# Seven-product MLP of a Hymba-style encoder block: a step's second weight load issued in its middle, shorter waits before the sums made ahead, four copies on ScalarE, and the third step's forms begun later

## The chip, the cores and the metric

The kernel runs on one core of one Trainium2 chip. The metric is device time in microseconds (us) of one execution. The kernel before took 2946.3 us (median of 3 runs, 2946.01 to 2948.02).

A core has five engines with a queue of instructions each, worked off in order: PE (TensorE: matrix products; its weight loads are listed apart as PEld), DVE (VectorE), ACT (ScalarE), POOL (GpSimd) and SP (SyncE, which here only issues transfers). An instruction that has to wait for another engine or a transfer holds up all that stands behind it in its own queue. Products are summed in PSUM banks; all other tiles lie in SBUF; "DRAM" is the chip's main memory.

## The reference, cut to what matters

The block mixes tokens (attention and a recurrent unit), adds the input, and then runs a gated MLP with a width-3 convolution along the sequence between its two projections. All numbers are float32. The change lies in the MLP:

```python
    h = rms_norm(x, norm2_g[l])                        # x: 2048 x 1024
    u = depthwise_conv(h @ w_up[l], up_conv_w[l], up_conv_b[l], 1, 1)   # w_up: 1024 x 6144
    gate, val = jnp.split(u, 2, axis=-1)
    x = x + (jax.nn.gelu(gate) * val) @ w_down[l]      # w_down: 3072 x 1024
return rms_norm(x, final_g)
```

## The kernel before, in words

**Seven products instead of eight.** Both projections are computed two blocks by two with seven block products in place of eight (a Strassen-like scheme). Each product takes sums and differences of the blocks as its operands, and its result is added to several blocks of the output. Every operand is held as two parts, a rounded one and the rest, so that a product is three passes of PE: high by high, high by low, low by high. Such a pair is a "form". `split` makes it: ACT writes the high part (line 142) and DVE subtracts (line 147).

**Steps.** There are 72 steps, i = 0 to 71. Steps 0 to 47 are the up-projection: 24 pairs of 128 columns (gate and value) for the second half of the sequence (steps 0 to 23) and for the first half (24 to 47; step 24 takes the forms of step 23, so nothing is loaded or formed for it). Steps 48 to 71 are the down-projection: three thirds q of the inner dimension, eight row pairs each. A step has seven *slots*, one for each product, of 12 matmuls each (four k by three passes), 84 in all (`mms`, line 1404). Products 0 to 3 have PSUM banks of their own; 4, 5 and 6 are added onto banks 0, 3 and 2 (`own = {4: 0, 5: 3, 6: 2}`). In slot 4 DVE adds bank 3 to an output block (`add(v2c, v2c, b[3])` in `step`, `add(x22, x22, b[3])` in `down`, both line 1485). PE's slot 5 writes onto bank 3 again, so its first matmul waits for this add.

**What a slot issues.** Behind its matmuls a slot queues, in this order: one piece of the step before (`before`: convolution, gelu, product, store), its own additions, one form of the next step (`nxt`, generator `a_forms`), and one piece of side work (`side`). An engine's queue is just the order of this code; nothing is reordered later.

**Forms of the next step.** Step i's weights (in the down-projection: the stored activations) come in two raw tiles, one for the columns of gate and one for those of value; a pool of three buffers (`rawp`) holds them. `load_w(i + 2)` is a generator that issues the first tile's load, yields, and issues the second's. Each goes out on SP's queue and waits there until its buffer is free. Steps i and i+2 need four tiles and the pool has three, so the second load of step i+2 waits until a_forms(i+1) has read its first tile for the last time: with the form of slot 4 in an up step, of slot 2 in a down step. POOL makes the sums of the raw tiles (lines 1314, 1316, 1318, 1322); the first of them reads the second tile.

**Side work.** The fixed operands also need sums. `sums_ahead` makes them from four loaded blocks of 128x512: it issues four loads, waits n slots, makes one sum a slot on DVE in four slots (lines 1596 to 1602), issues four stores two slots later, and ends: n + 8 slots in all. With n = 6 that is 14 slots, exactly two steps. There are four of these for the rows of the activations (names `h_d`, `t_d`) and twelve for the down-projection's weights (`in_w_down`, `wt_d`). They are chained from step 2 on (the four, then five) and from step 24 on (the other seven).

**Seams.** Where the fixed operand changes (steps 23, 47, 55 and 63) 28 forms are made anew during the step, four a slot (`remake`, tiles `fb<-rg`). They come through a ring of nine buffers (`load_ring`, tile `rg`). Nine loads are issued a step ahead; each further one is issued right behind a form, into the buffer which that form has freed.

**The first seam** is the start of the MLP: `emit_h2(0)` transposes the last rows on PE in four goes and copies each result out in two halves (ACT line 1219, DVE line 1220). The transposes have one PSUM buffer, so each waits for the copies of the one before.

The names of the page: `pu` is a bank of products, `fa` and `fb` are forms, `raw` the raw tiles, `s` POOL's sums, `y` and `u` the convolution's tiles, `x_t` a tile of the residual in the down-projection, `st` and `tp` the copies and transposes of `emit_h2`.

## Time and profile before

| | before |
|---|---|
| median of 3 runs | 2946.3 us |
| the profiled execution: time | 2942.63 us |
| its span, first to last instruction | 2940.8 us |
| mean granted TensorE clock | 0.979 |
| busy: PE, DVE, ACT, POOL | 2761.9, 2225.2, 1524.1, 710.5 us |
| first matmul of the MLP (tile `pu`) | 1410.1 us after the span's start |
| last one | starts at 2931.2 us |

The MLP is the second half of the span, 1521 us. Lines of a timeline read: start in us, duration in us, engine, line, operation, tiles out<-in, shapes, count, and in brackets how long the engine had been idle before and what ended that. "SPq" and "ACTq" are transfers being issued; the duration of such a row includes the waiting between the first and the last of its group. Lines of a list of waits read: who waited, for whom, total us, how many times, the longest.

### The profile page before, as it was taken

The page shows a single profiled execution, that of the slowest core. Times are in us where ns is not written, and L with a number is a line of the kernel's source. Part 1 is how long each engine was busy: PE and PEld are TensorE (multiplying, and loading weights), DVE is VectorE, ACT ScalarE, POOL GpSimd, SP SyncE. Part 2 cuts the span into 40 slices and gives each one's busy share as a digit, 9 for nine tenths or more (in the row PEclk, how much of TensorE's full clock was granted, in tenths as well). Part 3 has the DMA queues.
Part 4 walks back from the last instruction along what each step waited for, and adds up shares of the span by engine and source line. Part 5 has one row for each costly group of instructions (what it writes and reads, how often), then busy time and mean ns, then how long its engine had stood idle before and what let it go on. Part 6 is the DMA issues. An engine that isn't in the chain of part 4 may idle for free.

```text
span 2940.8 us, 34037 instructions
## 1 busy us (share of the span) xinstructions
PE 2761.9 (94%) x12016; PEld 2185.9 (74%) x12016; DVE 2225.2 (76%) x2954; ACT 1524.1 (52%) x2308; POOL 710.5 (24%) x576
## 2 busy tenths in 40 slices
PE   8998998999999999999799999989999979989898
PEld 6666786777777777777577777777777857868687
DVE  6766676888888888556778777787877777776776
ACT  5777534777777777434443434454444443232443
POOL 5224433111111111010032322212222223323221
PEclk9999998999999999999999999999999989989999
DMA  3233352111111111577333443444342245555653
GB/s 130 95 128 119 94 166 96 38 48 53 47 50 46 51 53 38 174 256 236 109 129 119 132 128 123 136 144 143 109 143 101 83 142 176 189 190 184 222 159 115
DMA packets 234171, 359.89 MB, mean 122 GB/s; under 512 B 30928, under 2 KB 119888, under 8 KB 233872
## 3 DMA queue, kind: packets, MB, share of 16 engines
q1 hardware_dynamic: 210960, 298.98, 32.4%
q10 hardware_dynamic: 23040, 58.73, 5.3%
q8 instruction: 94, 1.54, 0.2%
q14 instruction: 77, 0.63, 0.1%
HBM read 231.34 MB, written 118.42 MB: 119 GB/s over the span
## 4 chain that ended last, share of the span: by engine, by line
PE 54%; DVE 16%; DMA 6%; issue 4%; ACT 2%; SPq 1%; ACTq 0%; POOL 0%; DVEq 0%; POOLq 0%
PE pu L1404 31%; DVE u L1519 4%; PE mx L815 4%; PE s L975 4%; PE s L974 4%; PE b L1013 4%; PE b L1011 4%; PE a L1001 4%; DVE fa L147 2%; DMA b<-in_w_down 2%; PE po L1164 2%; DVE y L1485 2%; DVE fb L147 1%; SPq L90 1%; DMA l<-lru_d 1%
## 5 line engine op out<-in xcount | busy, mean ns | idle before, releaser
L1404 PE MATMUL pu<-fb,fa 128*128 128x512 f32 x6027 | 1412.5, 396 | 95.7 <-DVE y L1485 62.8
L1404 PEld LDWEIGHTS pu<-fb,fa 128*128 128x128 f32 x6027 | 1139.2, 190 | 366.9 <-DVE y L1485 73.0
L820 DVE TENSOR_REDUCE mxt<-mx 128x2 f32<-128x1024 f32 x244 | 298.3, 1223 | 82.0 <-PE mx L815 81.5
L1314 POOL TENSOR_TENSOR s<-raw 128x512 f32<-128x512 f32 x70 | 97.9, 1399 | 1038.8 <-DMA raw<-in_w_up 677.3
L984 ACT ACTIVATE phi<-s 128x1024 fp32r<-128x1024 f32 x256 | 263.2, 1028 | 153.3 <-PE s L975 145.9
L991 DVE TENSOR_TENSOR plo<-p,phi 128x1024 fp32r<-128x1024 f32 x256 | 332.1, 1298 | 7.9 <-ACT p L985 7.9
L147 DVE TENSOR_TENSOR fa<-raw,fa 128x512 fp32r<-128x512 f32 (+1 forms) x284 | 244.3, 860 | 100.7 <-ACT fa L142 99.7
L1519 DVE SCALAR_TENSOR_TENSOR u<-y,ucw_s,u 128x1024 f32<-128x1024 f32 (+1 forms) x192 | 264.5, 1378 | 1.7
L142 ACT ACTIVATE fa<-raw 128x512 fp32r<-128x512 f32 (+1 forms) x284 | 175.9, 620 | 171.3 <-PE pu L1404 90.1
L985 ACT ACTIVATE p<-s 128x1024 f32<-128x1024 f32 x256 | 261.3, 1021 | 0.5 <-DVE plo L991 0.3
L974 PE MATMUL s<-qa,ka 128*128 128x512 f32 x512 | 203.2, 397 | 4.2 <-ACT p L985 2.6
L975 PE MATMUL s<-qb,kb 65*128 65x512 f32 x512 | 203.5, 397 | 0.0
L147 DVE TENSOR_TENSOR fa<-s,fa 128x512 fp32r<-128x512 f32 (+1 forms) x213 | 157.9, 741 | 43.0 <-ACT fa L142 43.0
L1541 ACT ACTIVATE u<-u 128x1024 f32<-128x1024 f32 (+1 forms) x48 | 51.0, 1062 | 255.2 <-DVE u L1519 255.2
L815 PE MATMUL mx<-ka,qa 128*128 128x512 f32 x512 | 167.5, 408 | 11.9 <-DVE mxt L820 4.9
L1485 DVE TENSOR_TENSOR y<-pu,u 128x512 f32<-128x512 f32 x144 | 99.3, 690 | 102.6 <-PE pu L1404 102.4
L1164 PE MATMUL po<-wo_hi,m 128*128 128x512 f32 x512 | 167.2, 403 | 4.5 <-ACT fb L1029 3.7
L1528 ACT ACTIVATE u<-y,ucb_s,ucw_s 128x1024 f32<-128x1024 f32 (+1 forms) x96 | 119.2, 1242 | 98.9 <-DVE y L1485 97.1
L815 PEld LDWEIGHTS mx<-ka,qa 128*128 128x128 f32 x512 | 139.5, 310 | 40.0 <-DVE mxt L820 8.7
L142 ACT ACTIVATE fa<-s 128x512 fp32r<-128x512 f32 (+1 forms) x213 | 132.5, 622 | 57.0 <-PE pu L1404 31.9
L1013 PE MATMUL b<-phi,ones_r 128*65 128x512 f32 x512 | 161.2, 396 | 0.0
L1001 PE MATMUL a<-phi,vt 128*128 128x512 f32 x512 | 160.6, 395 | 0.0
(248 smaller groups left out, 4173.1 us busy)
## 6 DMA issues: line engine op xcount, KB each, us to landing
raw<-in_w_up SPq DMA_DIRECT2D x94, 512.0 KB
raw<-g_d SPq DMA_DIRECT2D x192, 128.0 KB
x_t<-x_d SPq DMA_DIRECT2D x96, 256.0 KB
x_t<-in_x SPq DMA_DIRECT2D x44, 512.0 KB
l<-lru_d SPq DMA_DIRECT2D x32, 512.0 KB
x_d<-x_t ACTq DMA_DIRECT2D x64, 256.0 KB
g_d<-u ACTq DMA_DIRECT2D x24, 512.5 KB
b<-in_w_down SPq DMA_DIRECT2D x48, 256.0 KB
```

Source lines behind the costliest of these rows:

```text
L142: ACT.activation(out=hi, in_=src, func=AF.Copy)
L147: e_lo.tensor_tensor(out=lo, in0=src, in1=f32(hi), op=ALU.subtract)
L815: PE.matmul(ps, lhsT=qa[u].rearrange("p (q t) -> p t q", t=4)[:, qt], rhs=ka[group(u)][:, kc * 512:(kc + 1) * 512], start=True, stop=True)
L820: DVE.tensor_reduce(out=mxt[u % 2][:, qt, 2 * kp:2 * kp + 2], in_=pair, axis=AX.X, op=ALU.max)
L974: PE.matmul(ps[:, h], lhsT=ka[g][:, keys], rhs=qa[u], start=True, stop=False)
L975: PE.matmul(ps[:, h], lhsT=kb[g][:, keys], rhs=qb[u], start=False, stop=True)
L984: ACT.activation(out=p_hi, in_=ps, func=AF.Exp)
L991: DVE.tensor_tensor(out=p_lo, in0=p, in1=f32(p_hi), op=ALU.subtract)
L1001: PE.matmul(pa[u], lhsT=vt[:, kt, group(u), 0:128], rhs=p_hi[:, h], start=kt == 0, stop=kt == 15)
L1013: PE.matmul(pb[u], lhsT=ones_r[:, 0:65], rhs=p_hi[:, h], start=False, stop=i == 7 and h == 1)
L1404: PE.matmul(ps, lhsT=lh, rhs=rh, start=start and n == 0, stop=stop and n == 2, skip_group_check=more)
L1519: DVE.scalar_tensor_tensor(out=u[:, 0:w], in0=y[:, o:o + w], scalar=ucw_s[:, t * FT + f, o:o + 1], in1=u[:, 0:w], op0=ALU.mult, op1=ALU.add)
```

## The change

Five edits:

1. `step`: `load_w(i + 2)` issues its first load at the step's start as before, and its second one in slot 4, behind that slot's form and ahead of its piece of side work.
2. `down`: the same in slot 3.
3. The twelve `sums_ahead` of the down-projection's weights wait n = 4 slots instead of 6; the four of the rows keep 6.
4. `emit_h2(0)`: both halves are copied by ACT; for the other row blocks nothing changes.
5. In step 1 the forms of step 2 begin three slots later; those that are left over come behind the step.

```diff
@@ emit_h2
                 ACT.activation(out=t[:, 0], in_=tp[:, 0], func=AF.Copy, scale=g2_s[:, k0:k0 + 1])
-                DVE.tensor_scalar(t[:, 1], tp[:, 1], g2_s[:, k0 + 1:k0 + 2], None, ALU.mult)
+                if v:
+                    DVE.tensor_scalar(t[:, 1], tp[:, 1], g2_s[:, k0 + 1:k0 + 2], None, ALU.mult)
+                else:
+                    ACT.activation(out=t[:, 1], in_=tp[:, 1], func=AF.Copy, scale=g2_s[:, k0 + 1:k0 + 2])
@@ step
-            run(load_w(i + 2))
+            ld = load_w(i + 2)
+            next(ld, None)
...
                 next(nxt, None)
+                if slot == 4:
+                    run(ld)
                 next(side, None)
@@
-        sums_w = [sums_ahead(down_srcs(n), wt_d[n], 6) for n in (8, 9, 10, 11, 4, 5, 6, 7, 0, 1, 2, 3)]
+        sums_w = [sums_ahead(down_srcs(n), wt_d[n], 4) for n in (8, 9, 10, 11, 4, 5, 6, 7, 0, 1, 2, 3)]
@@ down
-            run(load_w(i + 2))
+            ld = load_w(i + 2)
+            next(ld, None)
...
                 next(nxt, None)
+                if j == 3:
+                    run(ld)
                 next(side, None)
@@ the loop over the steps
-            nxt = a_forms(i + 1)
+            nxt = chain(wait(3), a_forms(2)) if i == 1 else a_forms(i + 1)
```

SP's queue in step 55, the seam between the first and the second third of the down-projection (`raw<-g_d` are quarters of a raw tile, `rg` ring loads):

```order
 L90 DMA raw<-g_d_119 128x2x128
 L90 DMA raw<-g_d_120 128x2x128
-L90 DMA raw<-g_d_121 128x2x128
-L90 DMA raw<-g_d_122 128x2x128
-L90 DMA raw<-g_d_123 128x2x128
-L90 DMA raw<-g_d_124 128x2x128
 L90 DMA rg<-wt_d_102 128x512
 L90 DMA rg<-wt_d_103 128x512
```

```order
-L90 DMA rg<-in_w_down 128x512 x8
+L90 DMA rg<-in_w_down 128x512 x5
+L90 DMA raw<-g_d_121 128x2x128
+L90 DMA raw<-g_d_122 128x2x128
+L90 DMA raw<-g_d_123 128x2x128
+L90 DMA raw<-g_d_124 128x2x128
+L90 DMA rg<-in_w_down 128x512 x3
```

The second raw tile's four loads stood ahead of all ring loads of the step and now stand behind twelve of them. In steps 23 and 47 (`step`, slot 4) the second load comes behind sixteen.

DVE's queue where the first sums of the weights are made, with n = 6 before (`t` and `b` are the sums, lines 1596 to 1602; `y_12721<-pu,y_12721` is the add of bank 3 in slot 4; of the change, the lines 1602 to 1608 and 1488 are the same instructions):

```order
L147 TENSOR_TENSOR fa<-raw,fa 128x512
L1596 TENSOR_TENSOR t_14306<-b 128x512
L1519 SCALAR_TENSOR_TENSOR u_12723<-y_12721,ucw_s,u_12723 128x1024 x2
L147 TENSOR_TENSOR fa<-s,fa 128x512
L1598 TENSOR_TENSOR b<-b 128x512
L1485 TENSOR_TENSOR u_12724<-pu,u_12724 128x512
L1519 SCALAR_TENSOR_TENSOR u_12722<-y_12720,ucw_s,u_12722 128x1024
L147 TENSOR_TENSOR fa<-raw,fa 128x512
L1600 TENSOR_TENSOR b<-t_14306,b 128x512
L1519 SCALAR_TENSOR_TENSOR u_12722<-y_12720,ucw_s,u_12722 128x1024
L1485 TENSOR_TENSOR y_12721<-pu,u_12724 128x512
L147 TENSOR_TENSOR fa<-s,fa 128x512
```

and of the change:

```order
L147 TENSOR_TENSOR fa<-s,fa 128x512
L1602 TENSOR_TENSOR t_14261<-b 128x512
L1488 TENSOR_TENSOR y_12720<-pu,u_12724 128x512
L147 TENSOR_TENSOR fa<-raw,fa 128x512
L1604 TENSOR_TENSOR b<-b 128x512
L1488 TENSOR_TENSOR y_12721<-pu,u_12724 128x512
L147 TENSOR_TENSOR fa<-raw,fa 128x512
L1606 TENSOR_TENSOR b<-t_14261,b 128x512
L1522 SCALAR_TENSOR_TENSOR u_12723<-y_12721,ucw_s,u_12723 128x1024 x2
L147 TENSOR_TENSOR fa<-s,fa 128x512
L1608 TENSOR_TENSOR b<-b 128x512
L1488 TENSOR_TENSOR u_12724<-pu,u_12724 128x512
```

Before, all four sums stand in slots 0 to 3 of a step, ahead of the add in slot 4. Now the first two stand in slots 5 and 6 of one step and the other two in slots 0 and 1 of the next. Since a chain link is 12 slots long instead of 14, the place moves two slots towards the step's start from link to link.

ACT's queue in step 1, before (`fa` are the forms of step 2, lines 1525 and 1528 the convolution of step 0, 1488 copies of a bank):

```order
L1488 ACTIVATE u_12724<-pu 128x512
L142 ACTIVATE fa<-s 128x512
L1525 ACTIVATE sv<-y_12721 128x2
L1528 ACTIVATE u_12723<-y_12721,ucb_s,ucw_s 128x1024
L142 ACTIVATE fa<-raw 128x512
L142 ACTIVATE fa<-s 128x512
L1525 ACTIVATE sv<-y_12720 128x2
```

and of the change:

```order
L1491 ACTIVATE u_12724<-pu 128x512
L1528 ACTIVATE sv<-y_12721 128x2
L1531 ACTIVATE u_12723<-y_12721,ucb_s,ucw_s 128x1024
L142 ACTIVATE fa<-raw 128x512
L1528 ACTIVATE sv<-y_12720 128x2
L1531 ACTIVATE u_12722<-y_12720,ucb_s,ucw_s 128x1024
L142 ACTIVATE fa<-s 128x512
```

The form of POOL's first sum (`fa<-s`) stood ahead of the convolution's two activations and now stands behind both.

## The prediction

> **What bounds the kernel now.** I read the page's engines first, then PE's waits, then PE's matmuls on `pu` in slices of 20 us, then the timeline at each stall.

> ```profile
> PE 2761.9 (94%) x12016; PEld 2185.9 (74%) x12016; DVE 2225.2 (76%) x2954; ACT 1524.1 (52%) x2308; POOL 710.5 (24%) x576
> PE pu L1404 <- DVE y L1485: 62.8, 19, 20.2
> PE pu L1404 <- DVE x_t L1485: 29.5, 3, 14.6
> 1540.00:1560.00 20.00, 18.38 (x81) 1.00 0.32 103
> 1560.00:1580.00 20.00, 20.00 (x89) 1.00 0.45 140
> 2400.00:2420.00 20.00, 4.45 (x20) 0.72 0.56 183
> 1490.76 19.18 PEld L1404 LDWEIGHTS pu<-fb,fa 128*128 128x128 f32 x84 [0.23 <-DVE y L1485]
> ```

> In the MLP PE is the bound: slices without a stall are full (20.00 of 20.00), and a step of 84 matmuls takes 19.2 us. What the change can win is PE's stalls, all behind adds on DVE (line 1485): 62.8 + 29.5 = 92.3 us. So for each stall the question is what made that add late. They fall into three kinds, with their rows below: one in about every second up step, one at each seam, one in step 1.

> **Sums of the weights (n = 4).** A step with four sums, then one without:

> ```profile
> 1496.59 0.69 DVE L1485 TENSOR_TENSOR y<-pu,u 128x512 f32<-128x512 f32 x1 [1.47 <-PE pu L1404]
> 1500.47 1.30 DVE L1596 TENSOR_TENSOR t<-b 128x512 f32<-128x512 f32 x1 [0.41 <-DMA b<-h_d]
> 1510.81 0.68 DVE L1602 TENSOR_TENSOR b<-b 128x512 f32<-128x512 f32 x1
> 1511.41 0.68 DVE L1485 TENSOR_TENSOR y<-pu,y 128x512 f32<-128x512 f32 x1
> 1512.14 10.19 PE L1404 MATMUL pu<-fb,fa 128*128 128x512 f32 x43 [1.79 <-DVE y L1485]
> 1864.65 0.69 DVE L1485 TENSOR_TENSOR y<-pu,u 128x512 f32<-128x512 f32 x1 [1.47 <-PE pu L1404]
> 1877.04 0.68 DVE L1485 TENSOR_TENSOR y<-pu,y 128x512 f32<-128x512 f32 x1
> ```

> The first `y<-pu,u` waits for the old step's last matmul and so marks the step's start; `y<-pu,y` is the add of slot 4. From one to the other's end: 1512.09 - 1496.59 = 15.50 with sums, 1877.72 - 1864.65 = 13.07 without. So a sum costs 2.43/4 = 0.61. PE wants the bank 60/84 of a step in, 13.7: a slack of 0.6 without sums, a stall of about 1.8 with four. The stall of 1.79 agrees.

> Of the 19 waits for `y`, three are seams (7.59, 6.13 and 20.15, quoted below); the other 16 make 62.8 - 33.9 = 28.9, or 1.81 each: 4 for the rows, 12 for the weights. Sums in slots 4 to 6 stand behind the add; DVE idles there (1.47 in the row above), so I count them as free. Their cost if that cover is gone: 0.61 each. With links of 12 slots a link starts in slot 0, 5, 3, 1, 6, 4, 2, and sums come 5 to 8 slots later, so 2, 1, 3, 3, 1, 2, 4 of the four lie in slots 0 to 3. At 0.61 less 0.6 that is 0.6, 0, 1.2, 1.2, 0, 0.6, 1.8. The five of the first half keep 3.0, the seven of the second 5.4: 8.4 in place of 12 x 1.81 = 21.7. **Gain 13**, bounds 5 (the backlog is carried into the next step) and 20. The rows keep n = 6 and their slots; only the 0.41 wait for `b` goes: **gain 1**, bounds -1 and 3.

> **The second load in the middle, up steps without a seam.**

> ```profile
> 1491.38 0.33 SPq L90 DMA_DIRECT2D raw<-in_w_up  x1
> 1491.75 2.20 SPq L90 DMA_DIRECT2D b<-h_d  x4
> 1495.59 1.30 POOL L1314 TENSOR_TENSOR s<-raw 128x512 f32<-128x512 f32 x1 [15.47 <-DMA raw<-in_w_up]
> 1496.97 1.29 POOL L1316 TENSOR_TENSOR s<-s,raw 128x512 f32<-128x512 f32 x1
> 1499.85 0.62 ACT L142 ACTIVATE fa<-s 128x512 fp32r<-128x512 f32 x1
> ```

> The second load goes out at 1491.38, 14 us into its step, when the form of slot 4 frees the buffer; the side's loads were queued in slot 0 and go out right behind. So the new place changes nothing for the second load, and the side's loads go out some 14 us sooner, which gives back more than n = 4 takes (two slots, 5.5 us). I cost it at 0. The cover: POOL's second sum ends at 1498.27 and ACT wants it at 1499.85, 1.6 us of room. Past that each us of delay is a us on DVE.

> **Seams of steps 47, 55 and 63.**

> ```profile
> 2407.87 3.98 SPq L90 DMA_DIRECT2D rg<-wt_d  x7
> 2411.87 1.32 ACT L142 ACTIVATE fb<-rg 128x512 fp32r<-128x512 f32 x2 [11.04 <-DMA rg<-wt_d]
> 2412.53 1.38 DVE L147 TENSOR_TENSOR fb<-rg,fb 128x512 fp32r<-128x512 f32 x2 [6.03 <-ACT fb L142]
> 2415.23 0.69 DVE L147 TENSOR_TENSOR fb<-rg,fb 128x512 fp32r<-128x512 f32 x1 [1.32 <-ACT fb L142]
> 2424.61 21.60 PE L1404 MATMUL pu<-fb,fa 128*128 128x512 f32 x83 [20.15 <-DVE y L1485]
> 2448.19 2.11 PE L1404 MATMUL pu<-fb,fa 128*128 128x512 f32 x8 [1.76 <-DVE x_t L1485]
> 2574.98 2.49 DVE L147 TENSOR_TENSOR fb<-rg,fb 128x512 fp32r<-128x512 f32 x4
> 2586.93 0.69 DVE L147 TENSOR_TENSOR fb<-rg,fb 128x512 fp32r<-128x512 f32 x1 [7.12 <-ACT fb L142]
> 2588.85 1.36 DVE L147 TENSOR_TENSOR fb<-rg,fb 128x512 fp32r<-128x512 f32 x2 [1.23 <-ACT fb L142]
> 2591.93 5.71 DVE L147 TENSOR_TENSOR fb<-rg,fb 128x512 fp32r<-128x512 f32 x4
> 2592.10 1.65 POOL L1314 TENSOR_TENSOR s<-raw 128x512 f32<-128x512 f32 x1 [23.11 <-DMA rg<-in_w_down]
> 2598.30 13.94 PE L1404 MATMUL pu<-fb,fa 128*128 128x512 f32 x49 [14.59 <-DVE x_t L1485]
> 2758.08 0.69 DVE L147 TENSOR_TENSOR fb<-rg,fb 128x512 fp32r<-128x512 f32 x1 [6.84 <-ACT fb L142]
> 2768.68 26.52 PE L1404 MATMUL pu<-fb,fa 128*128 128x512 f32 x103 [13.15 <-DVE x_t L1485]
> ```

> In step 47 the ring loads go out only at 2407.87, behind the second raw load, which waits for slot 2's form. ACT then waits 11.04 for the tenth ring tile, and DVE idles 6.03 + 1.32 = 7.35. Moved behind the ring loads, the raw load no longer holds them up; a ring load goes out nine forms (over two slots) before its own form, and the first landed 4.0 after its issue (2407.87 to 2411.87). So DVE's idle time goes.

> Step 47: DVE stays the bound through slot 4 of step 48, where PE waits 1.76 again. The stall in 47 shrinks by about 10, that in 48 grows, and together they win DVE's idle time. **Gain 7**, bounds 3 and 11.

> Step 55: idle 7.12 + 1.23 = 8.35. Besides, the four forms of slot 3 took 5.71 while POOL was summing, against 2.49 without: 3.2 more. POOL will start later than those forms, since the raw load now lands behind twelve ring loads. The add comes 8.35 + 3.2 = 11.6 sooner, the stall falls from 14.6 to 3.0. The 3.2 return in slots 4 to 6 and may cost about 1 in step 56. **Gain 10.5**, bounds 6 and 14. Step 63 is alike: 6.84 + 0.5 + 3.2 = 10.5 of 13.15. **Gain 10**, bounds 6 and 13.

> The clock: after 20.15 us without work 83 matmuls took 21.60, 2.4 more than a step's 19.2, at a granted 0.72; after stalls of 1.8 it stayed at 1.00. I leave this out of the sum, as a stall of 3 lies between. [...]

> **Step 23.**

> ```profile
> 1923.17 23.05 PE L1404 MATMUL pu<-fb,fa 128*128 128x512 f32 x90 [6.13 <-DVE y L1485]
> 1905.90 3.29 DVE L147 TENSOR_TENSOR fb<-rg,fb 128x512 fp32r<-128x512 f32 x4 [1.93 <-ACT fb L142]
> ```

> The ring wasn't held up here (its second raw buffer is free early). The raw load moves behind sixteen ring loads, and POOL's sums from slot 0 (3.29 instead of 2.49) to the seam's end. **0**: 0.8 won, as much lost later; bounds -3 and 1.

> **The first seam and step 1.**

> ```profile
> 1426.43 0.48 DVE L1220 TENSOR_SCALAR st<-tp,g_s 128x256 f32<-128x256 f32 x1
> 1426.96 1.11 PE L1216 MATMUL tp<-idn,x_t 128*128 128x128 f32 x4 [4.94 <-DVE st L1220]
> 1460.17 0.63 ACT L142 ACTIVATE fa<-s 128x512 fp32r<-128x512 f32 x1 [4.81 <-POOL s L1316]
> 1460.83 1.11 DVE L147 TENSOR_TENSOR fa<-s,fa 128x512 fp32r<-128x512 f32 x1 [5.08 <-ACT fa L142]
> 1469.38 11.00 PE L1404 MATMUL pu<-fb,fa 128*128 128x512 f32 x38 [7.59 <-DVE y L1485]
> ```

> PE waits 4.94 for DVE's half of a copy (1426.43); ACT's second copy would follow its first, some 2.5 sooner, for 0.5 more of ACT each. **Gain 2**, bounds 0 and 3. In step 1 ACT waits 4.81 for POOL with the convolution queued behind, DVE 5.08, and PE 7.59. With the forms three slots later the convolution goes first, and about 5.5 of the 7.59 go; three forms (1.8 on DVE) then lie ahead of step 2, and its second raw load waits for one of them. **Gain 5**, bounds 1 and 7.

> **Sum.** 13 + 1 + 7 + 10.5 + 10 + 0 + 2 + 5 = 48.5. From the profiled execution's 2942.6: 2894.1. That run lies 3.7 below the median of 2946.3, so the forecast is 2898.

> **Rivals.**
> - *The sums merely move their stall.* DVE works nearly without a pause in a side step; a sum in slots 5 and 6 could delay the next step's add. Against it: the idle 1.47, and the step after each one with sums makes no stall. Gain 0 in place of 13: 2911.
> - *The seams stay bound.* 28 forms of 0.6 us each are work for DVE all the same, and the ring could be late for its own reasons. For it: the stall of 6.13 in step 23, where nothing holds up the ring. Against it: DVE's idle 7 to 8 us. A third of 27.5 is left: 2916.
> - *Slower: the second load is late.* It now queues in SP behind the side's stores, which wait for DVE's sums, and loads, which wait for those stores. The place: up steps 2 to 36 in which both are emitted in slots 0 to 3. It decides once those are held until more than 1.6 us past the buffer's release, 14 us into the step. In about ten such steps a load 8 us late (the time from the issue of four `b` at 1491.75 to the first sum) costs 6.4 each, 64, less the seams' and step 1's 35: 2975. Against it: their sums stand a slot or more ahead of the form that frees the buffer, so the wait is over first. [...]
> - *The clock returns.* If PE keeps its full clock after a stall of 3, as it does after 1.8, the 2.4 us lost after a long one are saved at 55 and at 63: 2893.

> **Chances.** Forecast 0.58, sums 0.10, seams 0.12, clock 0.12, slower 0.08. Range 2882 to 2924: the independent bounds of the terms (about 12 either way around 48.5), stretched to take in the first two rivals and a mix of them; without them 2886 to 2910. What a measurement can tell from no change is about 0.2%, 6 us. Only the slower case and a sliver of the mixes lie outside "faster": 0.90, same 0.03, slower 0.07.

> **What would show it.** Right: no DVE idle behind ring loads in the seams, stalls of about 10 and 6 in steps 47 and 48 and about 3 in 55 and 63; in the second half of the up steps stalls of 0 to 1.8 that differ from link to link, in the rows' steps still 1.8; a stall of about 2 in step 1. Wrong: ACT waiting for POOL's `s` in up steps (the load is late); `rg` still named as releaser in the seams; stalls of 1.8 in every link, or small ones in every step.

## The result, and the profile after

The changed kernel takes 2912.9 us (median of 4 runs, 2911.99 to 2916.96) where the kernel before takes 2946.2 us on the same chip (4 runs, 2944.01 to 2948.02): a ratio of 0.989, 95% interval 0.9873 to 0.9907. The forecast was 2898, with a range of 2882 to 2924. So it is faster, and inside the range, but only 33 of the 48.5 us came. The time is outside 2886 to 2910, the bounds of the terms alone, and nearer to two of the rivals (2911 and 2916) than to the forecast; whether one of them was at work has to be read from the stretches below.

The profiled execution of the changed kernel took 2917.0 us, with a span of 2915.2. The busy times from its page and the list of PE's waits (who waited for whom, total us, times, longest):

```profile
PE 2770.3 (95%) x12016; PEld 2191.9 (75%) x12016; DVE 2232.0 (77%) x2950; ACT 1525.6 (52%) x2312; POOL 713.6 (24%) x576
```

```profile
PE pu L1407 <- DVE y L1488: 43.9, 21, 9.8
PE pu L1407 <- DVE x_t L1488: 17.7, 5, 5.3
```

The lines of the changed kernel are three higher: 1407 are the matmuls, 1488 DVE's adds, 1317 to 1325 POOL's sums, 1522 the taps of the convolution. PE's waits for these adds went from 62.8 + 29.5 = 92.3 us to 61.6.

**Where the time went.** ScalarE copies bank 0 once in every step (`u<-pu`, 72 of them), so these copies are a ruler along the program. From the timeline of the kernel before, the first matmul into `pu` and the copies of the steps 5, 23, 25, 47, 49, 57 and 71:

```profile
1410.11 1.61 PE L1404 MATMUL pu<-fb,ax 128*128 128x512 f32 x6 [0.87 <-DVE x_t L1170]
...
1540.07 0.60 ACT L1488 ACTIVATE u<-pu 128x512 f32<-128x512 f32 x1 [0.17 <-PE pu L1404]
...
1907.34 0.57 ACT L1488 ACTIVATE u<-pu 128x512 f32<-128x512 f32 x1
1953.14 0.60 ACT L1488 ACTIVATE u<-pu 128x512 f32<-128x512 f32 x1 [0.21 <-PE pu L1404]
...
2395.24 0.57 ACT L1488 ACTIVATE u<-pu 128x512 f32<-128x512 f32 x1
2456.83 0.60 ACT L1488 ACTIVATE u<-pu 128x512 f32<-128x512 f32 x1 [4.80 <-PE pu L1404]
2628.60 0.60 ACT L1488 ACTIVATE u<-pu 128x512 f32<-128x512 f32 x1 [4.83 <-PE pu L1404]
2915.18 0.58 ACT L1488 ACTIVATE u<-pu 128x512 f32<-128x512 f32 x1
```

and of the changed kernel:

```profile
1417.46 1.84 PE L1407 MATMUL pu<-fb,ax 128*128 128x512 f32 x7 [0.88 <-DVE x_t L1170]
...
1545.17 0.60 ACT L1491 ACTIVATE u<-pu 128x512 f32<-128x512 f32 x1 [0.17 <-PE pu L1407]
...
1904.88 0.58 ACT L1491 ACTIVATE u<-pu 128x512 f32<-128x512 f32 x1
1953.99 0.60 ACT L1491 ACTIVATE u<-pu 128x512 f32<-128x512 f32 x1 [0.21 <-PE pu L1407]
...
2387.62 0.58 ACT L1491 ACTIVATE u<-pu 128x512 f32<-128x512 f32 x1
2442.14 0.60 ACT L1491 ACTIVATE u<-pu 128x512 f32<-128x512 f32 x1 [4.80 <-PE pu L1407]
2607.31 0.60 ACT L1491 ACTIVATE u<-pu 128x512 f32<-128x512 f32 x1 [4.84 <-PE pu L1407]
2889.94 0.58 ACT L1491 ACTIVATE u<-pu 128x512 f32<-128x512 f32 x1
```

Each start less that of the first matmul, before minus after, gives what is won up to there; the difference of two such numbers is what a stretch wins. The last column is a second profiled execution of the same kernel, from the experiments below.

| stretch (from copy to copy) | terms of the prediction | forecast, us | won | won, second execution |
|---|---|---|---|---|
| start to step 5 | copies, third step's forms | 7 | 2.2 | 2.2 |
| 5 to 23 | rows, five links of the weights | 7 | 7.6 | 8.1 |
| 23 to 25 | step 23 | 0 | -3.3 | -5.5 |
| 25 to 47 | seven links of the weights | 7.3 | 8.5 | 9.5 |
| 47 to 49 | seam 47 | 7 | 7.1 | 6.1 |
| 49 to 57 | seam 55 | 10.5 | 6.6 | 7.4 |
| 57 to 71 | seam 63 | 10 | 4.0 | 5.3 |
| sum | | 48.5 | 32.6 | 33.1 |

(The weights' 13.3 had been rounded to 13.)

The first matmul itself came at 1410.1, 1417.5 and 1411.9: the part ahead of it, which is the same program, differs by several us from one execution to another. So below, beside the median of the runs, the ruler is used: it leaves that part out.

**The first steps.** From the timeline of steps 1 and 2:

```profile
1468.29 21.18 PE L1407 MATMUL pu<-fb,fa 128*128 128x512 f32 x84 [4.16 <-DVE y L1488]
...
1482.34 1.49 POOL L1317 TENSOR_TENSOR s<-raw 128x512 f32<-128x512 f32 x1 [13.58 <-DMA raw<-in_w_up]
1482.59 4.55 DVE L1522 SCALAR_TENSOR_TENSOR u<-y,ucw_s,u 128x1024 f32<-128x1024 f32 x2
...
1486.09 0.63 ACT L142 ACTIVATE fa<-s 128x512 fp32r<-128x512 f32 x1 [3.66 <-POOL s L1319]
...
1494.72 5.46 PE L1407 MATMUL pu<-fb,fa 128*128 128x512 f32 x12 [5.25 <-DVE y L1488]
```

The stall of step 1 fell from 7.59 to 4.16, but step 2 now stalls for 5.25 where it had 0.23. Its second raw load is late, POOL starts its sums in the middle of the convolution, two taps take 4.55 beside them, and ACT waits 3.66 for POOL.

**The seams.** Step 55 and the step behind it, from the timeline:

```profile
2572.95 13.92 PE L1407 MATMUL pu<-fb,fa 128*128 128x512 f32 x48 [3.94 <-DVE x_t L1488]
...
2579.82 4.70 DVE L147 TENSOR_TENSOR fb<-rg,fb 128x512 fp32r<-128x512 f32 x4
...
2588.05 0.68 DVE L1488 TENSOR_TENSOR x_t<-pu,x_t 128x512 f32<-128x512 f32 x1
2588.88 15.41 PE L1407 MATMUL pu<-fb,fa 128*128 128x512 f32 x59 [2.00 <-DVE x_t L1488]
```

The stall in slot 5 fell from 14.59 to 3.94, close to the 3.0 forecast. But 48 matmuls, four slots, later PE stalls again for 2.00: that is slot 2 of step 56, which needs bank 2. The add that frees bank 2 (2588.05) completes an output block of step 55, but is queued in slot 0 of step 56, behind all forms of step 55. Four of these forms took 4.70 while POOL was summing (2.49 alone). In step 63 the pair is 5.32 and 3.31.

### The profile page after: what moved, and what is told of

The parts are those of the page before. It is cut to its first block, busy times and chain, and to the rows that moved or that the text cites. A ratio compares the mean times of both kernels' runs of the same rounds, so it can differ in the third digit from the quotient of the medians.

```text
span 2915.2 us, 34136 instructions
## 1 busy us (share of the span) xinstructions
PE 2770.3 (95%) x12016; PEld 2191.9 (75%) x12016; DVE 2232.0 (77%) x2950; ACT 1525.6 (52%) x2312; POOL 713.6 (24%) x576
## 3 DMA queue, kind: packets, MB, share of 16 engines
q8 instruction: 94, 1.54, 0.2%
## 4 chain that ended last, share of the span: by engine, by line
PE 60%; DVE 13%; DMA 4%; issue 3%; ACT 2%; SPq 0%; DVEq 0%; ACTq 0%
PE pu L1407 35%; PE mx L815 4%; PE s L975 4%; PE s L974 4%; PE b L1013 4%; PE b L1011 4%; PE a L1001 4%; PE po L1164 3%; DVE u L1522 3%; DVE fb L147 2%; DVE fa L147 1%; DVE y L1488 1%; DMA sc<-sig_d 1%; DVE mxt L820 1%; DMA l<-lru_d 1%
## 5 line engine op out<-in xcount | busy, mean ns | idle before, releaser
L147 DVE TENSOR_TENSOR fa<-raw,fa 128x512 fp32r<-128x512 f32 (+1 forms) x284 | 244.2, 860 | 106.9 <-ACT fa L142 102.2
L142 ACT ACTIVATE fa<-raw 128x512 fp32r<-128x512 f32 (+1 forms) x284 | 176.1, 620 | 181.7 <-PE pu L1407 89.5
L147 DVE TENSOR_TENSOR fa<-s,fa 128x512 fp32r<-128x512 f32 (+1 forms) x213 | 161.0, 756 | 38.9 <-ACT fa L142 38.6
L142 ACT ACTIVATE fa<-s 128x512 fp32r<-128x512 f32 (+1 forms) x213 | 132.6, 622 | 59.9 <-PE pu L1407 32.6
```

The source lines that it names most:

```text
L142: ACT.activation(out=hi, in_=src, func=AF.Copy)
L147: e_lo.tensor_tensor(out=lo, in0=src, in1=f32(hi), op=ALU.subtract)
```

## The experiments

The kernel before ran beside each group on the same chip: 2943.5 us beside the two runs of one edit alone, the forms at once and step 23; 2944.1 beside the changed kernel again, the later link, the seams' loads last and the stores on SP; 2942.6 beside the run without POOL's sums and the two combined ones. Ratios are against these.

### The changed kernel again

No edit.

> The changed kernel once more, unchanged, so that the runs beside it can be compared with it on the same chip. Expected 2912, 1.1% below the kernel before; its up and down steps alone, from the first matmul into pu to the end, 33 us less than the kernel before, whatever the part ahead of them takes.

2911.4 us, ratio 0.9892 (0.9877 to 0.9907); the ruler gives 33.1 us less than before. The size of the result stands; single stretches at the seams differ by 1 to 2 us between the two executions.

### One edit alone: the later second load

In the kernel before:

```
-            run(load_w(i + 2))
+            ld = load_w(i + 2)
+            next(ld, None)
...
+                if slot == 4:      # in down: if j == 3
+                    run(ld)
                 next(side, None)
```

> The kernel before with one edit alone: the second load of each up and down step in the step's middle. Theory from the two traces: nothing in the ordinary up steps (the links still make stalls of about 1.8), a loss of 3.3 in step 23 and 24, gains of 7.1, 6.6 and 4.3 at steps 47, 55 and 63: 14.7 in all, 2931.5. The prediction's sizes (rival): 27.5 at the three seams, 2919. Second rival: the sums' gain is owed to the side's loads that now go out sooner, and the stalls of 1.8 shrink here already: 2920 or less, and the seams are as in the theory.

2926.6 us, 16.9 less, ratio 0.9942 (0.9930 to 0.9955); by the ruler 16.5 less: up to step 23 it loses 1.6, the stretch 23 to 25 loses 5.0, steps 25 to 47 win 2.7, and the stretches of the seams 47, 55 and 63 win 7.7, 8.8 and 3.8. The theory holds in the main (14.7 expected): alone, this edit is worth its seams. The links' stalls stay, 0.80 to 1.68 in steps 25 to 37, so the second rival falls.

### One edit alone: shorter waits before the weights' sums

In the kernel before:

```
-        sums_w = [sums_ahead(down_srcs(n), wt_d[n], 6) for n in (8, 9, 10, 11, 4, 5, 6, 7, 0, 1, 2, 3)]
+        sums_w = [sums_ahead(down_srcs(n), wt_d[n], 4) for n in (8, 9, 10, 11, 4, 5, 6, 7, 0, 1, 2, 3)]
```

> The kernel before with one edit alone: four slots in place of six between a link's loads and its first sum, weights only. If the place of the sums among DVE's work is all that counts, it wins what the two traces show between steps 11 and 46, about 15: 2931. If the sooner loads are needed for it (in the kernel before, the side's loads go out behind the second raw load, 14 us into the step), DVE waits for b at the first sum in the links that start in slots 0 to 3, and the gain is between 0 and 8: 2938 to 2946.

2962.3 us, 18.8 *more* than before, ratio 1.0062 (1.0049 to 1.0075); the ruler gives 22.2 more. Neither expectation had that sign. DVE's waits (for the same data 6.2 in all, 8 times, in the kernel before), and a link in the timeline:

```profile
DVE t L1596 <- DMA b<-in_w_down: 32.0, 7, 7.2
```

```profile
1659.30 1.86 SPq L90 DMA_DIRECT2D b<-in_w_down  x4
...
1667.61 1.40 DVE L1596 TENSOR_TENSOR t<-b 128x512 f32<-128x512 f32 x1 [7.05 <-DMA b<-in_w_down]
```

The four loads still go out late in the step, behind the second raw load. The first sum, two slots earlier in DVE's queue, stands there and waits 7.05 for its data, with the convolution and the bank adds behind it. In the changed kernel no sum waits for `b` in the list of DVE's waits.

So the two edits are not two terms. Alone they make -16.9 and +18.8, +1.9 in all; the edits of the first steps add some -2 to -3; the changed kernel has -33. Some 32 us exist only when both are there. On top of the later loads, though, n = 4 is worth what was forecast for it: against the run with the loads alone, the two executions of the changed kernel win 14.0 and 15.6 more in the stretches 5 to 23 and 25 to 47.

### The first steps: forms at once, and the side's link later

The changed kernel with the third step's forms at their old place:

```
-            nxt = chain(wait(3), a_forms(2)) if i == 1 else a_forms(i + 1)
+            nxt = a_forms(i + 1)
```

> The changed kernel with the third step's forms back at their old place (its other edits kept). From the trace of the changed kernel (the theory): delaying the forms took 3.4 us from the stall of step 1 (7.59 to 4.16) and put 5.0 us into step 2 (0.23 to 5.25), so undoing it wins about 2 us: 2911, with a stall of about 7.5 in step 1 and below 1 in step 2. The prediction's term (the rival): the delay wins 5, so undoing it costs 5: 2918, with 7.5 in step 1 and step 2 as in the changed kernel without the delay's help. If the loss in step 2 comes from the later second load and not from the forms, step 2 still stalls by 2 or more here.

2910.4 us, ratio 0.9885 (0.9870 to 0.9901): by the runs not to be told from the changed kernel. By the ruler, 1.0 is won up to step 5, against 2.2 with the delay. So the delayed forms win about 1: the 5 of the prediction is wrong, and so is the theory above, that they lose. Step 2 stalls here as well, for another reason:

```profile
1470.28 1.85 SPq L90 DMA_DIRECT2D b<-h_d  x4
...
1472.14 0.33 ACTq L90 DMA_DIRECT2D g_d<-u  x1
...
1479.55 1.25 ACT L1531 ACTIVATE u<-y,ucb_s,ucw_s 128x1024 f32<-128x1024 f32 x1 [3.85 <-DMA g_d<-u]
...
1485.77 14.52 PE L1407 MATMUL pu<-fb,fa 128*128 128x512 f32 x55 [2.43 <-DVE y L1488]
```

The side's first loads now go out at 1470.28, ahead of the store of the convolution's result. The store lands late, and ACT, which writes the same tile for the next step, waits 3.85 for it. To test this, the same kernel with the side begun six slots later:

```
+            if i == 2:
+                side = chain(wait(6), side)
             what = remake(changes[i]) if i in changes else side
```

> The changed kernel, with the third step's forms at their old place and the side's first link six slots later (its loads no longer go out ahead of the store of the first convolution's result). Theory: in the run with the forms at their old place the side's four loads, issued at 1470.28 ahead of the store g_d<-u at 1472.14, made the store late; the next convolution waited 3.85 for it, and PE stalled 2.43 in step 2, which swallowed the 3.4 won by the first seam's copies. Here ACT does not wait for the store, step 2 stalls by under 1, and the steps up to step 4 gain about 3.5 against the kernel before (1.0 with the forms at their old place alone): 2909. Rival: the late store is due to the raw loads that SP issues at the same time, the wait stays, and it equals the run with the forms at their old place: 2911 to 2913.

```profile
1465.33 46.95 PE L1407 MATMUL pu<-fb,fa 128*128 128x512 f32 x193 [7.63 <-DVE y L1488]
...
1475.16 0.33 ACTq L90 DMA_DIRECT2D g_d<-u  x1
1475.88 1.23 ACT L1531 ACTIVATE u<-y,ucb_s,ucw_s 128x1024 f32<-128x1024 f32 x1
...
1487.91 2.02 SPq L90 DMA_DIRECT2D b<-h_d  x4
```

2906.6 us, ratio 0.9875 (0.9860 to 0.9890). ACT doesn't wait for the store, PE runs 193 matmuls, over two steps, without a stall, and the copy of step 4 comes 4.6 sooner than before (1.0 with the forms at once alone). Part of that is a stall put off: the link's own, 1.79 in step 3 before, now comes behind that copy with 1.19, and at step 5 the gain is 3.1 (1.0). The theory holds. Edit 4 is worth 2.8 to 3.4 up to the copy of step 0 (0.2 and 0.4 in the two runs without it), and with the forms at once the side's early loads took it back.

### Step 23

The changed kernel, with step 23's second load at its start:

```
             ld = load_w(i + 2)
             next(ld, None)
+            if i == FT - 1:
+                run(ld)
```

> The changed kernel, with the second load of step 23 alone back at the step's start. Theory: the load behind the ring's loads moved POOL's sums onto the forms at the seam's end, which cost the two extra stalls of 1.50 and 2.57 in step 24; undone, step 23 stalls by about 6 once, step 24 not at all, and the kernel is 3.3 faster: 2909.6. Rival: the extra stalls come from the links' earlier sums or from the tiles of the ring, and nothing changes: 2913.

```profile
1889.10 1.29 POOL L1317 TENSOR_TENSOR s<-raw 128x512 f32<-128x512 f32 x1 [14.28 <-DMA raw<-in_w_up]
...
1910.61 31.76 PE L1407 MATMUL pu<-fb,fa 128*128 128x512 f32 x129 [6.26 <-DVE y L1488]
```

2904.2 us, ratio 0.9868 (0.9855 to 0.9882). POOL makes its sums ahead of the seam's forms, at 1889.10, and behind the stall of 6.26 PE runs on through step 24 without another. The stretch 23 to 25 wins 0.1 where the changed kernel loses 3.3 and 5.5, as the theory had it. Of the 6 to 7 us by which the ratio is better than the changed kernel's, the ruler shows 1.0 to 1.6 (34.1 won in all), since the seam at 55 won 6.5 here and seam 63 3.2 up to the last copy. The rest is not explained by the edit; in the profiled execution the first matmul came at 1406.9, 5 to 10.6 sooner than in those of the changed kernel.

### The seams: what makes the second stall

First, in the four seam steps the second load after the ring's last load:

```
-                if slot == 4:      # in down: j == 3
+                if slot == 4 and i not in changes:
                     run(ld)
                 next(side, None)
+                if slot == 6:
+                    run(ld)
```

> The changed kernel, with the second load of the four seam steps (23, 47, 55, 63) after the last load of the ring, at the end of slot 6. Theory: POOL's four sums leave the seam's last forms (which took 4.08, 5.78 and 4.70 beside them, 1.9 to 2.5 alone), and the ring's last loads are not held up; the second stalls of 1.50, 1.67, 2.00 and 3.31 in slot 2 of steps 24, 48, 56 and 64 go, 8 in all: 2904. Rival: POOL's sums then come too late for the first forms of the next step, ACT waits there for POOL's s by 2 to 4 us at each seam, and what is won is lost again: 2910 to 2920.

2901.1 us, ratio 0.9858 (0.9842 to 0.9875); 41.2 by the ruler. Step 55:

```profile
2576.06 2.49 DVE L147 TENSOR_TENSOR fb<-rg,fb 128x512 fp32r<-128x512 f32 x4
...
2583.70 0.63 ACT L142 ACTIVATE fa<-s 128x512 fp32r<-128x512 f32 x1 [5.75 <-POOL s L1319]
...
2589.63 2.58 PE L1407 MATMUL pu<-fb,fa 128*128 128x512 f32 x10 [1.54 <-DVE x_t L1488]
```

The last forms take 2.49 again, and the stall in slot 2 is gone. The rival's wait is there too (ACT waits 5.75 for POOL's sums), but it costs PE only 1.54. The stretches to 57 and to 71 win 9.4 and 8.4. Step 23 isn't mended: it still loses 3.2, now because POOL's sums lie beside the taps of step 24.

Two things moved in that run: POOL's sums left the forms, and the raw load left the ring's last loads. So POOL's four sums of steps 25, 49, 57 and 65 were left out, and with them a part of the computation, with the load where the changed kernel has it:

```
             g, v = raws.pop(i)
+            if i - 2 in (FT - 1, UP - 1, UP + NV - 1, UP + 2 * NV - 1):
+                for t in (v[:, 0:512], v[:, 512:1024], g[:, 512:1024], g[:, 0:512], v[:, 0:512], g[:, 512:1024], v[:, 512:1024]):
+                    yield t
+                return
```

> The changed kernel, with POOL's four sums of the steps 25, 49, 57 and 65 left out (the forms of these steps are made from the raw weights as loaded, so part of the computation is left out). The second load stays in the seam's middle, ahead of the ring's last loads. It tells apart what the later load removed at the seams: POOL's work beside DVE's forms, or the raw load's place ahead of the ring's last tiles. If POOL's work is the cause (theory): the seam's last forms take 2.5 for four, the second stalls in slot 2 of steps 24, 48, 56 and 64 go, and it is about 10 faster than the changed kernel: 2901. If the load's place is the cause: ACT still waits for the ring's last tiles, the second stalls stay, and it takes 2909 to 2912.

```profile
2565.81 24.39 PE L1411 MATMUL pu<-fb,fa 128*128 128x512 f32 x94 [5.05 <-DVE x_t L1492]
...
2571.09 2.49 DVE L147 TENSOR_TENSOR fb<-rg,fb 128x512 fp32r<-128x512 f32 x4
```

2900.1 us, ratio 0.9857 (0.9843 to 0.9870). In steps 55 and 63 no second stall is left; the stretches to 49, 57 and 71 win 10.8, 9.4 and 8.2. So at 47, 55 and 63 it is POOL's work beside DVE's forms, not the load's place in the queue. At step 23 it is not POOL alone: without its sums the stretch 23 to 25 still loses 3.3, with ACT waiting for the ring's last tiles:

```profile
1923.79 1.30 ACT L142 ACTIVATE fb<-rg 128x512 fp32r<-128x512 f32 x2 [1.34 <-DMA rg<-t_d]
...
1925.92 0.63 ACT L142 ACTIVATE fb<-rg 128x512 fp32r<-128x512 f32 x1 [0.83 <-DMA rg<-t_d]
```

A third suspect was ScalarE's issue of the `x_d` stores, which ACT and DVE seemed to wait for:

```
-                            dma(out=row_tile(i, r)[0][:, c * 512:c * 512 + 512], in_=x[r][c], eng=ACT)
+                            dma(out=row_tile(i, r)[0][:, c * 512:c * 512 + 512], in_=x[r][c],
+                                eng=SP if i + 1 in changes else ACT)
```

> The changed kernel, with the four x_d stores that ScalarE issues in slot 2 of steps 55 and 63 issued on SP instead. Theory: ScalarE's issue of them is slow while SP issues the ring's loads (2.98 and 4.35 for three, 1.80 and 1.41 in the kernel before), ACT and DVE wait for it (DVE 1.61 and 2.99), and that is why the stalls of 3.94 and 5.32 are not about 1 shorter and 3 shorter: about 4 us faster, 2908, with stalls of about 2.5. Rival: the four issues hold up the ring's loads on SP by as much, ACT waits for rg instead, and nothing changes: 2912, or worse by up to 4.

2912.4 us, ratio 0.9888 (0.9869 to 0.9907), no change. Step 63:

```profile
2733.11 11.32 PE L1407 MATMUL pu<-fb,fa 128*128 128x512 f32 x48 [2.24 <-DVE x_t L1488]
...
2739.22 6.87 DVE L147 TENSOR_TENSOR fb<-rg,fb 128x512 fp32r<-128x512 f32 x4
...
2750.44 5.03 PE L1407 MATMUL pu<-fb,fa 128*128 128x512 f32 x11 [6.01 <-DVE x_t L1488]
```

The first stall fell to 2.24, as the theory had it, and the second rose to 6.01: the forms then met POOL's sums in full (6.87 for four). In step 55 the pair is 2.24 and 5.06. What is won ahead of such a collision is lost in it.

### Together

The changed kernel with the forms at once, the side six slots later, step 23's load at its start, and the loads of 47, 55 and 63 last; then the same with n = 4 for the rows too:

```
-        side = chain(*[sums_ahead(rows_srcs(k), t_d[k], 6) for k in range(4)], *sums_w[:5])
+        side = chain(*[sums_ahead(rows_srcs(k), t_d[k], 4) for k in range(4)], *sums_w[:5])
```

> The changed kernel with what the runs so far favour: the third step's forms at their old place, the side's first link six slots later, step 23's second load at the step's start, the second loads of steps 47, 55 and 63 after the ring's last load. If these add up, against the changed kernel's steps: 4.2 (forms and link) + 3.2 (step 23) + 1.4 + 2.0 + 4.0 (47, 55, 63) = 14.8: 2896.5. If they share a cause, less: 2901.

> The same, and the rows' sums four slots behind their loads too, as the weights' are. The four rows' links still make stalls of 1.2 to 1.6 (5.0 in all); by the placement that held for the weights they shrink to a third: 3 faster than the run without it, 2893.5. Rival: the rows' loads land later than the weights' (they lie behind the stores of the copies and the raw loads), DVE waits for b, and nothing is won.

2898.4 us (ratio 0.9852, 0.9838 to 0.9867) and 2895.5 us (0.9842, 0.9829 to 0.9856); the ruler gives 44.6 and 46.5. The second is the fastest of all, faster than both kernels: its interval lies below that of the changed kernel. The gains added up nearly as expected (44.6 - 33.1 = 11.5 of 14.8). The step from 6 to 4 for the rows is 1.9 by the ruler, less than an interval. Step 63 of the last run, with no second stall in the 159 matmuls that follow:

```profile
2721.31 38.88 PE L1407 MATMUL pu<-fb,fa 128*128 128x512 f32 x159 [5.72 <-DVE x_t L1488]
```

## Why the prediction was right and wrong

**Sums of the weights and rows: 14 forecast, 16.0 and 17.6 measured.** The size is right and rests on the right mechanism: the sums' place among DVE's work. The links show it one by one. For the seven of the second half the prediction had stalls of 0.6, 0, 1.2, 1.2, 0, 0.6 and 1.8; in the steps where their sums stand (25, 26, 28, 30, 32, 33 and 35) they were 0.59, none, 0.94, 1.18, 0.18, 0.61 and 1.31. The first rows of PE there (252 matmuls are three steps):

```profile
1965.58 58.62 PE L1407 MATMUL pu<-fb,fa 128*128 128x512 f32 x252 [0.59 <-DVE y L1488]
2025.14 38.90 PE L1407 MATMUL pu<-fb,fa 128*128 128x512 f32 x168 [0.94 <-DVE y L1488]
2065.23 38.92 PE L1407 MATMUL pu<-fb,fa 128*128 128x512 f32 x168 [1.18 <-DVE y L1488]
```

So the rival that the sums merely move their stall did not hold, though its 2911 is near the time. What was wrong is to book the gain to one edit. The prediction put 13 on n = 4 and 0 on the later second load. It did say that the side's loads then go out some 14 us sooner, "which gives back more than n = 4 takes", but as a remark, not as the condition of the 13. With it n = 4 wins 14.0 and 15.6, without it n = 4 is a loss of 18.8. A condition under which a term holds is part of the term.

**The second load late (the slower rival).** It didn't come. In the up and down steps of the changed kernel ACT waits for POOL's sums `s` twice, 6.8 in all, in steps 1 and 2; the step behind a side's store is not among them.

**Step 47: 7 forecast, 7.1 and 6.1 measured.** Right, stalls included: 9.78 in step 47 against "about 10", and two of 1.67 and 3.15 in step 48 against one of 6.

**Steps 55 and 63: 20.5 forecast, 10.6 and 12.7 measured.** The first half held: in the seams 47, 55 and 63 DVE had waited 23.0 in all for forms out of the ring, and no such wait is left (ACT still waits 9.0 for ring tiles, 29.4 before); the first stall fell to 3.9 and 5.3. The step that failed is "The 3.2 return in slots 4 to 6 and may cost about 1 in step 56". They return onto the add that frees bank 2, which the prediction did not follow: it looked only at bank 3. The price is a stall of 2.0 and 3.3 in slot 2 of the next step, and each is followed by 3.41 us at a granted clock of 0.50, with 8 and 10 matmuls where the next 3.41 us at 1.00 have 16. With POOL's sums out of the way, in two different manners, the two seams win 17.6 to 17.8, so this one term is worth about 5 to 7 of the 8 to 10 missing us. The rest is a first stall 0.9 and 2.7 longer than the 3.0 and 2.65 forecast. The run with the `x_d` stores on SP, where it was 2.24 in both steps, puts that on ScalarE's issue of these stores, which the prediction did not count. The rival that the seams stay bound (a third of 27.5 left, 2916) did not hold either: the three seams won 17.6 and 18.8, about two thirds, and for the reasons given here.

**Step 23: 0 forecast, -3.3 and -5.5 measured, bounds -3 and 1.** "0.8 won, as much lost later" failed. The load was free of trouble at the step's start; moved, it puts itself ahead of the ring's last three tiles, or, moved further, POOL's sums beside the taps of step 24. Either costs 3 or more.

**The first seam and step 1: 7 forecast, 2.2 measured.** The copies won 3.4 and 2.9, more than the 2. The forms' 5 failed at "three forms (1.8 on DVE) then lie ahead of step 2, and its second raw load waits for one of them": this was named and priced at 1.8, and cost most of what step 1 won (step 2 stalls for 5.25). With the forms at their old place step 2 loses 3.5 instead (from its copy to the next), because the side's loads go out sooner, which the prediction counted as harmless, and ACT waits for a store behind them. In the changed kernel itself no wait for that store is listed. No run has the delayed forms together with the later link, so what the delay alone is worth stays open.

**The clock rival.** It said that stalls of 3 would leave the clock alone. They were 3.94 and 5.32, so its condition was not met, and they cost the clock. Behind the stall of 3.94 in step 55 (stretch, its length, PE busy, matmuls, granted clock, DMA share, GB/s):

```profile
2573.00:2577.00 4.00, 4.00 (x10) 0.50 1.00 308
```

After 3.94 us the clock is at 0.50. A second fall to 0.50 came after the stall of only 2.00 in step 56; that one is taken up in the last section. The prediction's 0.72 is the mean of 2400 to 2420, most of it stall; over the matmuls behind the stall, 2424.61 to 2446.21, the clock was 0.89.

## What to carry to other kernels

Ask of every term under which condition it holds, and whether another edit of the same change supplies or removes that condition: two edits that make -17 and +19 us alone made some -31 together. When a stall shrinks, follow the late engine to the *last* thing it owes in that step, here the add of bank 2, since a backlog that is carried over came due there (stalls of 2.00 and 3.31). And a load that goes out sooner was not free here (ACT waited 3.85 for a store behind it): ask which store or load behind it lands later, and who waits for that.

## What was new of the hardware

Four DVE subtractions of a form take 2.49 us alone; beside POOL's sums they took 4.70 and 5.78 (changed kernel, steps 55 and 47) and 6.87 (stores on SP, step 63), two taps 4.55 in place of 2.59 (changed kernel, step 2), and POOL's own sums 1.6 to 3.2 in place of 1.3. With POOL's sums left out, the four of step 55 took 2.49 again. Why the two engines slow each other down is not shown by a run here. What was not expected is how much hangs on where it falls: without the sums the stretches at 47, 55 and 63 won 2.5 to 4.2 more than the changed kernel (mean of its two executions), while the same sums a few us later, in step 56, cost PE 1.54.

In the changed kernel's trace stalls of 3.94 and more lowered the granted clock to 0.50, and so did those of 2.00 (step 56) and 3.31 (step 64). Those of 2.57 (step 24) and 3.15 (step 48) did not. So the length of a stall alone doesn't decide it. No run was made to test what does; what follows is measured in the traces of the two kernels from 1450 us on. The stretches at half clock last 3.41, 6.83, 10.24, 13.65, 17.07 or 20.48 us, whole multiples of 3.413 (but for the last of each trace, which runs past the last instruction), and within a trace all changes of the clock lie whole multiples of 3.413 us apart, to 0.01. So a trace can be cut into windows of that length with every change at a bound. Here are the changed kernel's windows around the stall of 2.00 and around that of 3.15, in the same columns; PE idles for what its busy time leaves of the length:

```profile
2585.46:2588.88 3.42, 1.42 (x8) 1.00 0.81 227
2588.88:2592.29 3.41, 3.41 (x8) 0.50 0.57 199
...
2428.45:2431.86 3.41, 1.89 (x9) 1.00 0.19 53
2431.86:2435.27 3.41, 1.78 (x8) 1.00 0.91 252
```
